# MLP products of a diffusion layer: eight half-sized block products against seven, in two phases

## The chip, the core and the metric

The kernel runs on one core of a Trainium2 chip. The metric is device time in microseconds (us) of one execution, as the median of three runs. Everything is float32. A product of two float32 operands is made of three TensorE passes: each operand is split into a rounded part (hi, type float32r) and the rest (lo), and hi·hi, hi·lo and lo·hi are added up in PSUM.

## What is computed

One layer over 512 latent tokens (and 256 context tokens) with 2048 features: modulated RMSNorm, a combined input projection that feeds three kinds of mixers, an output projection with gated residual, and then the part that this change is about, the MLP and the final norm:

```python
def _sq_relu_mlp(h, w1, w2):                      # h (512, 2048), w1 (2048, 8192), w2 (8192, 2048)
    a = jax.nn.relu(jnp.einsum('btd,df->btf', h, w1))
    return jnp.einsum('btf,fd->btd', a * a, w2)

# h = modulate(rmsnorm(x2), ...);  x = x2 + gate * mlp(h);  out = rmsnorm(x)
```

## The kernel before

TensorE holds 128x128 of one operand (the weight load, `PEld`) and streams columns of the other through it. `mm3` (L169 to L172) issues the three passes of a product, each with a weight load of its own.

Until about 1230 us of the profile the kernel does conditioning, input projection, mixers and output projection; the change leaves these as they are, but for the buffers that the output projection's end uses. Then come:

- The turn to the MLP (L921 to L946). `flip` scales and transposes the tokens `x2` by matmuls with the diagonal `dg` into PSUM tiles `pt`; ScalarE applies the modulation (`hf`, L944), VectorE rounds it into `hh` (L945), VectorE and GpSimd in turn form the rest `hl` (L946).
- The MLP loop over 8 groups of 1024 hidden units (`for g in range(NG)`, L950). In a group, 8 tiles of 128 hidden units are made from w1: the weights are held, `hh` and `hl` stream with 512 columns (all tokens), 16 row tiles by 3 passes into one PSUM bank `pa`. The bank goes through relu and square, and is split into `ah` and `al`, which stay in SBUF. Then the group's 1024 rows of w2 are used: `ah`/`al` are held (128 tokens), w2 streams with 512 columns into banks `yp`, and `add_up` multiplies by the gate `gb2` (L996) and adds into the residual `x2` (L997, on GpSimd).
- Both use `wunit` (L97): a unit is 128x1024 float32 (512 KB), loaded by SyncE's queue into one of three buffers `raw`, rounded on ScalarE (`whi`, L93) and subtracted on VectorE (`wlo`, L94), each with two buffers. `wunit` runs at a raised priority (`WPRI`), so the planner puts it ahead of other work of the same engine. Each engine executes its instructions in the order that the planner wrote.
- In the last group three of the four token tiles are finished first (`LASTM`), and the row of the fourth ends the kernel: gate, residual, sum of squares, `row_rstd`, scaling, two output DMAs (L1005 to L1010).

In all, w1 takes 64 tiles x 16 row tiles x 3 = 3072 matmuls of 512 columns and w2 the same number.

Of the kernel before, what the change touches and what calls it, by code (L numbers as in the profile page):

```python
# [9 lines left out]
F32 = mybir.dt.float32  # L10
# [7 lines left out]
P = 128  # L18
# [23 lines left out]
LASTM = (0, 1, 2)  # L42
GT = 8
# [5 lines left out]
def trunk_kernel(ctx: ExitStack, tc: tile.TileContext, a: dict, out: bass.AP, dbg: dict):  # L49
    """Products of float32 operands run as float32r passes: each operand is split exactly into  # L50
    hi (rounded to float32r) and lo = operand - hi, and hi*hi + hi*lo + lo*hi is accumulated."""
# [14 lines left out]
    gd = [dram.tile([P, 512], F32, name=f"gd{i}") for i in range(4)]  # L66

# [29 lines left out]
    def wunit(src, n, p=WPRI, after=None, into=None):  # L97
        """one unit of weights, loaded and split; `after` holds the load back until that is there"""
# [46 lines left out]
    def row_store(blk, ac):  # L145
        pb = mx.tile([P, 512], F32, tag="mx", name="pb")
        TE.matmul(pb, onem, ac, start=True, stop=True)
        S.copy(ac, pb)
        G.dma_start(out=gd[blk], in_=ac)
# [24 lines left out]
    def log1pexp(pool, tag, x, shape):  # L174
        """ln(1 + exp(-|x|))"""
# [6 lines left out]
    def rsqrt_into(y, t, v):  # L182
        """y = v ** -0.5: exponential of half the logarithm, then one Newton step"""
# [15 lines left out]
    hp = ctx.enter_context(tc.tile_pool(name="hT", bufs=1, side="right"))  # L199
# [14 lines left out]
    def col_rstd(rb, t, total, pb, n, start):  # L214
        """rsqrt of the mean over the features of every token's squares, on every partition"""
# [11 lines left out]
    with tc.tile_pool(name="pa", bufs=1) as pa:  # L227
# [8 lines left out]
        # four columns (c hi, c_ctx hi, c lo, c_ctx lo), repeated over the array's width  # L236
# [155 lines left out]
    def hg_b2(h, chain, mods):  # L392
        """q and output gate, feature-major"""
# [78 lines left out]
    def hg_gates(outs, tiles, toks):  # L472
        """log forget and key, token-major [tok, tile, fw|bw]"""
# [668 lines left out]
```

## Time and profile before

| | |
|---|---|
| median of three runs (lowest, highest) | 2671.26 us (2670.48, 2672.54) |
| span of the profiled execution | 2665.3 us |
| TensorE busy, weight loads busy | 98%, 84% |
| VectorE, ScalarE, GpSimd busy | 48%, 32%, 12% |
| moved by DMA | 349.61 MB, mean 131 GB/s |

The profiled execution is one of its own; between its span and the median of the runs lie 6.0 us, which hold what is before the first and after the last instruction. Ends of matmuls are modelled and overlap the next one, so a matmul's duration (0.39 us for 512 columns) is not its price; the price is the distance from one start to the next.

### The profile page before, as it was taken

What the parts mean: (1) busy time and instruction counts of PE and PEld (TensorE: products, weight loads), DVE (VectorE), ACT (ScalarE), POOL (GpSimd) and SP (SyncE); (2) the same over time, 40 slices, a digit from 0 to 9 for tenths busy, and PEclk for the clock granted to TensorE, in tenths of its full rate; (3) what the DMA queues carried; (4) which work ended last, traced back from release to release, by engine and by line L of the source; (5) the groups of instructions that cost most, each with busy time, mean ns of one, the idle gap of its engine ahead of it and who ended that gap; (6) DMA issues with size and microseconds to landing.
All of it is one profiled execution on the core that took longest, in us unless ns stands there. A gap on an engine that the chain in (4) does not pass through costs nothing.

```text
span 2665.3 us, 33283 instructions
## 1 busy us (share of the span) xinstructions
PE 2619.2 (98%) x13498; PEld 2248.4 (84%) x13498; DVE 1281.1 (48%) x1900; ACT 864.4 (32%) x1279; POOL 314.8 (12%) x301
## 2 busy tenths in 40 slices
PE   8999999999999999999999999999999999999998
PEld 6879999998999988787888888888888888888886
DVE  8885666755444556566333333333333333333345
ACT  7664445522222234223222212222122222221233
POOL 0030000001001010002011020120200201102014
PEclk9999999999999999999999999999999999999999
DMA  9843333435455464663322222222222222223234
GB/s 330 295 166 113 108 117 109 131 103 182 132 164 149 157 188 152 219 201 125 99 97 95 95 96 99 98 95 95 95 97 99 98 95 95 96 97 100 95 119 150
DMA packets 101099, 349.61 MB, mean 131 GB/s; under 512 B 15280, under 2 KB 15536, under 8 KB 100304
## 3 DMA queue, kind: packets, MB, share of 16 engines
q1 hardware_dynamic: 90000, 322.09, 36.3%
q0 software_dynamic: 10944, 25.39, 3.1%
q8 instruction: 106, 1.74, 0.3%
q14 instruction: 49, 0.40, 0.0%
HBM read 336.37 MB, written 11.01 MB: 130 GB/s over the span
## 4 chain that ended last, share of the span: by engine, by line
PE 79%; DMA 9%; DVE 7%; ACT 2%; issue 2%; POOL 1%; SPq 0%; DVEq 0%; ACTq 0%; POOLq 0%
PE pa L170 9%; PE pa L172 9%; PE pa L171 9%; PE yp L171 9%; PE yp L172 9%; PE yp L170 8%; DMA raw<-in_ada_dram 8%; DVE adac L119 3%; DVE wlo L94 2%; PE f L170 2%; PE f L171 2%; PE f L172 2%; PE vP L170 1%; PE vP L171 1%; PE vP L172 1%
## 5 line engine op out<-in xcount | busy, mean ns | idle before, releaser
L94 DVE TENSOR_TENSOR wlo<-raw,whi 128x1024 fp32r<-128x1024 f32 (+1 forms) x452 | 551.0, 1220 | 874.6 <-ACT whi L93 873.8
L93 ACT CAST whi<-raw 128x1024 fp32r<-128x1024 f32 (+1 forms) x452 | 466.0, 1036 | 1221.4 <-PE yp L172 564.9
L170 PE MATMUL pa<-hh,whi 128*128 128x512 f32 x1024 | 402.8, 393 | 0.0
L172 PE MATMUL pa<-hh,wlo 128*128 128x512 f32 x1024 | 401.8, 392 | 0.0
L171 PE MATMUL pa<-hl,whi 128*128 128x512 f32 x1024 | 398.0, 389 | 0.0
L171 PE MATMUL yp<-wlo,ah 128*128 128x512 f32 x960 | 373.9, 389 | 1.3 <-DVE wlo L94 1.3
L170 PE MATMUL yp<-whi,ah 128*128 128x512 f32 x960 | 373.9, 389 | 0.0
L172 PE MATMUL yp<-whi,al 128*128 128x512 f32 x960 | 373.6, 389 | 0.0
L997 POOL TENSOR_TENSOR x<-x,yt 128x512 f32<-128x512 f32 x124 | 190.0, 1562 | 1183.7 <-DVE yt L996 1170.1
L119 DVE SCALAR_TENSOR_TENSOR adac<-raw,csil,adac 128x512 f32<-128x512 f32 x256 | 192.0, 750 | 246.7 <-DMA raw<-in_ada_dram 237.4
L172 PEld LDWEIGHTS pa<-hh,wlo 128*128 128x128 f32 x1024 | 192.3, 188 | 44.5 <-DVE wlo L94 0.3
L171 PEld LDWEIGHTS pa<-hl,whi 128*128 128x128 f32 x1024 | 192.2, 188 | 43.5 <-POOL hl L946 0.3
L170 PEld LDWEIGHTS pa<-hh,whi 128*128 128x128 f32 x1024 | 192.5, 188 | 38.8
L171 PEld LDWEIGHTS yp<-wlo,ah 128*128 128x128 f32 x960 | 180.2, 188 | 40.0 <-DVE wlo L94 2.5
L170 PEld LDWEIGHTS yp<-whi,ah 128*128 128x128 f32 x960 | 180.2, 188 | 37.8 <-ACT whi L93 0.4
L172 PEld LDWEIGHTS yp<-whi,al 128*128 128x128 f32 x960 | 180.2, 188 | 37.5
L996 DVE TENSOR_TENSOR yt<-yp,gb 128x512 f32<-128x512 f32 x128 | 85.3, 687 | 51.2 <-PE yp L172 47.1
L170 PE MATMUL f<-whi,hh 128*128 128x384 f32 x256 | 90.7, 354 | 3.2 <-ACT whi L93 3.2
L171 PE MATMUL f<-wlo,hh 128*128 128x384 f32 x256 | 87.2, 341 | 0.6 <-DVE wlo L94 0.6
L172 PE MATMUL f<-whi,hl 128*128 128x384 f32 x256 | 86.9, 339 | 0.0
L170 PE MATMUL vP<-whi,hh 128*128 128x256 f32 x256 | 74.0, 289 | 0.0
L276 PE MATMUL ga<-whi,cw 128*128 128x256 f32 x256 | 66.4, 293 | 7.5 <-ACT whi L93 7.5
(365 smaller groups left out, 4330.1 us busy)
## 6 DMA issues: line engine op xcount, KB each, us to landing
raw<-in_w_dram SPq DMA_DIRECT2D x264, 512.0 KB, 3.5
raw<-in_ada_dram SPq DMA_DIRECT2D x192, 512.0 KB, 4.2
raw<-in_nb_dram SPq DMA_DIRECT2D x48, 512.0 KB, 3.5
raw<-in_wo_dram SPq DMA_DIRECT2D x32, 512.0 KB, 3.6
raw<-in_hb_dram SPq DMA_DIRECT2D x32, 384.0 KB, 3.1
wr<-in_hq_dram SPq DMA_DIRECT2D x16, 384.0 KB, 4.5
raw<-in_hb_dram SPq DMA_DIRECT2D x12, 512.0 KB, 3.5
xT<-in_xT_dram SPq DMA_DIRECT2D x4, 1024.0 KB, 11.1
```

What stands on the lines that cost most here:

```text
L93: S.copy(hi[:, :n], raw)
L94: V.tensor_sub(lo[:, :n], raw, hi[:, :n].bitcast(F32))
L119: V.scalar_tensor_tensor(ac, raw[:, kk * 512:(kk + 1) * 512], csil[:, 2 * u + kk:2 * u + kk + 1], ac, op0=ALU.mult, op1=ALU.add)
L170: TE.matmul(o, lh, rh, start=start, stop=False, skip_group_check=skip)
L171: TE.matmul(o, lh, rl, start=False, stop=False, skip_group_check=skip)
L172: TE.matmul(o, ll, rh, start=False, stop=stop, skip_group_check=skip)
L276: TE.matmul(ga[:, :256], st, hi[:, cs], start=(n == 0), stop=False)
L996: V.tensor_mul(t_, yp[m], gb2[:, cs])
L997: (V if end else G).tensor_add(x2[:, m, cs], x2[:, m, cs], t_)
```

## The change

The matrices of each product are cut in halves: the tokens in two times 256, the inner dimension in two, and the weights' columns in two. A block product of 2x2 by 2x2 blocks would take eight products of blocks. The new kernel makes seven, named N1 to N7, of sums of blocks; a fixed order (`visits`) interleaves two neighbouring blocks.

- Weights. N1, N2 and N3 load a block as it is (b11, b21, b22). N5, N6 and N4 use the buffer of N1 again: a DMA that GpSimd issues adds b12, then b22, then b21 onto what is there; N7 adds b12 onto the buffer of N3. Each of the seven is then split as before (`Weights.split`). The extra buffers are 3 raw and 3 split pairs in the first phase, 8 and 3 in the second.
- Phase 1 (w1): 32 blocks of 256 hidden units. A visit is 8 row tiles x 3 passes of 256 columns into one of the banks X, Y, Z; N6, N7 and N4 continue the sum that stands in bank X, N3 that in Y. After each visit ScalarE or VectorE takes the bank's state out. After N4: relu, square, four sums (`combine`), and a split into the seven operands of the next phase, which two DMAs write to DRAM (`acd`).
- Phase 2 (w2): 16 blocks of 512 hidden units by 1024 columns. A visit has two units of weights and two token tiles, 24 matmuls of 512 columns, and its operand (1 MB) is loaded from `acd` on every second block. After each visit VectorE adds to or subtracts from `y` (128x512, twice).
- The residual `x2` is kept in DRAM (`x2d`), and gate, residual and final norm come after the last block (`gate`, `finish_row`).
- The MLP's input is combined in the same way: for each of 8 pairs of row tiles two modulations, `combine`, and two splits (`hah`/`hal` 1024, `hbh`/`hbl` 768 columns).

```diff
-        hf = mlp.tile([P, T], F32R, tag="ah", name="hf", bufs=11).bitcast(F32)
-        S.activation(hf, pt.rearrange("p m t -> p (m t)"), AF.Identity, bias=mod[:, 0, k:k + 1], scale=mod[:, 1, k:k + 1])
-        V.tensor_copy(hh[:, k], hf)
-        (G if k % 2 else V).tensor_sub(hl[:, k], hf, hh[:, k].bitcast(F32))
+    def combine(x):
+        G.tensor_sub(x[:, 3], x[:, 6], x[:, 7])
+        V.scalar_tensor_tensor(x[:, 0], x[:, 3], -1.0, x[:, 4], op0=ALU.mult, op1=ALU.subtract)
+        G.tensor_sub(x[:, 1], x[:, 4], x[:, 7])
+        V.scalar_tensor_tensor(x[:, 2], x[:, 0], -1.0, x[:, 5], op0=ALU.mult, op1=ALU.subtract)
...
+        if k < 8:
+            hx = hc.tile([P, 8, 256], F32, tag="hx", name="hx", bufs=3)
+        S.activation(hx[:, 4:8:3] if k < 8 else hx[:, 5:7], pt, AF.Identity, bias=mod[:, 0, k:k + 1], scale=mod[:, 1, k:k + 1])
+        if k >= 8:
+            combine(hx)
+            S.copy(hah[:, :, p], hx[:, 3:7])
+            V.tensor_sub(hal[:, :, p], hx[:, 3:7], hah[:, :, p].bitcast(F32))
+            S.copy(hbh[:, :, p], hx[:, 0:3])
+            V.tensor_sub(hbl[:, :, p], hx[:, 0:3], hbh[:, :, p].bitcast(F32))
...
+        def operand(self, blk, name, src, held):
+            b11, b12, b21, b22 = src
+            with pri(WPRI):
+                if name in ("N1", "N2", "N3"):
+                    t = held[name] = self.raw()
+                    nc.sync.dma_start(out=t, in_={"N1": b11, "N2": b21, "N3": b22}[name])
+                else:
+                    t, add = {"N5": (held["N1"], b12), "N6": (held["N1"], b22), "N7": (held.get("N3"), b12),
+                              "N4": (held["N1"], b21)}[name]
+                    G.dma_start(out=t, in_=add, accum_op=ALU.add)
+                return self.split(t)
+
+    def visits(n):
+        out_ = [(0, "N1"), (0, "N5")]
+        for b in range(n):
+            more = b + 1 < n
+            out_ += [(b, "N2"), (b, "N3"), (b, "N6")] + [(b + 1, "N1")] * more + [(b, "N7")]
+            out_ += [(b + 1, "N5")] * more + [(b, "N4")]
+        return out_
...
+    for q, name in visits(32):
...
+        for k in range(8):
+            xh, xl = h_op(PLACE[name], k)
+            mm3(b_, wh[:, k], wl[:, k], xh, xl, new and k == 0, k == 7, skip=True)
+        with pri(EPRI):
+            if name in ("N1", "N5", "N3"):
+                r = made[q, name] = p1.tile([P, 256], F32, tag="r", name="r", bufs=4)
+                if name == "N1":
+                    S.copy(r, b_)
+                else:
+                    S.activation(r, b_, AF.Copy, scale=-1.0)
+            elif name == "N2":
+                ac[q] = p1.tile([P, 8, 256], F32, tag="ac", name="ac", bufs=1)
+                V.tensor_add(ac[q][:, 4], made[q, "N1"], b_)
+            elif name == "N6":
+                V.tensor_sub(ac[q][:, 5], made[q, "N3"], b_)
+            elif name == "N7":
+                V.tensor_sub(ac[q][:, 6], made[q, "N5"], b_)
+            else:
+                S.copy(ac[q][:, 7], b_)
+        if name == "N4":
+            x = ac[q]
+            S.activation(x[:, 4:8], x[:, 4:8], AF.Relu)
+            S.activation(x[:, 4:8], x[:, 4:8], AF.Square)
+            combine(x)
...
+            S.copy(xh, x[:, 0:7])
+            V.tensor_sub(xl, x[:, 0:7], xh.bitcast(F32))
+            for i, y in enumerate((xh, xl)):
+                nc.sync.dma_start(out=acd[q // 4].rearrange("o p i b t -> p o i b t")[:, :, i, q % 4], in_=y.bitcast(F32))
...
+    for b, name in visits(nb):
+        if j == 0:
+            t = aops[g, name] = p2.tile([P, 2, 4, 256], F32R, tag="ao", name="ao", bufs=8)
+            with pri(WPRI):
+                nc.sync.dma_start(out=t.bitcast(F32), in_=acd[g][PLACE[name]])
...
+                    mm3(bank[b, which][m], t[:, 0, i, sl], t[:, 1, i, sl], wh[:, kk], wl[:, kk], new and i == 0, i == 3, skip=True)
...
+        with pri(EPRI):
+            for m in range(2):
+                o = y[:, half + m, cs]
+                src = bank[b, which][m]
+                if first:
+                    S.activation(o, src, AF.Copy, scale=float(sign))
+                else:
+                    (V.tensor_add if sign > 0 else V.tensor_sub)(o, o, src)
```

## Rows read from the trace of the kernel before

**Rows 1.** The page: span, busy time of the engines, and its slices.

```profile
span 2665.3 us, 33283 instructions
...
PE 2619.2 (98%) x13498; PEld 2248.4 (84%) x13498; DVE 1281.1 (48%) x1900; ACT 864.4 (32%) x1279; POOL 314.8 (12%) x301
...
PEclk9999999999999999999999999999999999999999
```

**Rows 2.** Waits, 1200 to 2665 us: who waited, us in total, times, longest.

```profile
ACT whi L93 <- PE yp L172: 495.8, 119, 4.8
...
ACT whi L93 <- DMA raw<-in_w_dram: 10.2, 3, 4.9
```

**Rows 3.** The timeline of TensorE: first and last matmuls of the MLP.

```profile
1250.46 0.48 PE L170 MATMUL pa<-hh,whi 128*128 128x512 f32 x1
...
2653.52 0.40 PE L172 MATMUL yp<-hh,al 128*128 128x512 f32 x1
```

**Rows 4.** The timeline of TensorE where 256 columns stream: two runs of matmuls.

```profile
900.20 0.28 PE L171 MATMUL vP<-wlo,hh 128*128 128x256 f32 x1
...
901.34 0.28 PE L172 MATMUL vP<-whi,hl 128*128 128x256 f32 x1
...
902.16 0.28 PE L170 MATMUL vP<-whi,hh 128*128 128x256 f32 x1
...
904.90 0.28 PE L172 MATMUL vP<-whi,cl 128*128 128x256 f32 x1
```

**Rows 5.** Stretches: us, busy time by engine, granted clock, DMA share, GB/s.

```profile
10.00:20.00 10.00, 8.99 (x38) 5.64 (x37) 6.02 (x8) 7.85 (x15) 0.00 (x0) 1.00 1.01 424
...
50.00:60.00 10.00, 10.00 (x69) 9.18 (x68) 8.65 (x11) 7.11 (x9) 0.00 (x0) 1.00 0.96 355
...
1700.00:1800.00 100.00, 100.00 (x442) 82.63 (x441) 35.27 (x37) 21.59 (x22) 24.23 (x16) 1.00 0.29 95
```

**Rows 6.** Groups by line and shape, 1250 to 2660 us: busy, mean ns, idle before.

```profile
L94 DVE TENSOR_TENSOR wlo<-raw,whi 128x1024 fp32r<-128x1024 f32 x254 | 318.0, 1252 | 788.3 <-ACT whi L93 788.3
L93 ACT CAST whi<-raw 128x1024 fp32r<-128x1024 f32 x254 | 267.7, 1054 | 913.8 <-PE yp L172 482.2 <-PE pa L171 421.5 <-DMA raw<-in_w_dram 5.3
...
L996 DVE TENSOR_TENSOR yt<-yp,gb 128x512 f32<-128x512 f32 x128 | 85.3, 687 | 51.2 <-PE yp L172 47.1 <-POOL x L997 4.1
...
L962 ACT ACTIVATE rl<-pa 128x512 f32<-128x512 f32 x64 | 37.7, 589 | 0.0
```

**Rows 7.** The same view of 0 to 700 us and of GpSimd: smaller shapes.

```profile
L94 DVE TENSOR_TENSOR wlo<-raw,whi 128x768 fp32r<-128x768 f32 x32 | 30.5, 953 | 13.3 <-ACT whi L93 13.3
L93 ACT CAST whi<-raw 128x768 fp32r<-128x768 f32 x32 | 26.6, 830 | 57.0 <-PE f L172 47.6 <-DVE st L622 9.3
...
L352 POOL TENSOR_TENSOR cl<-cx,ch 128x256 fp32r<-128x256 f32 x8 | 7.1, 889 | 0.5 <-DVE cl L352 0.5
```

**Rows 8.** DMA issues: queue, count, KB each, median us to landing.

```profile
raw<-in_w_dram SPq DMA_DIRECT2D x264, 512.0 KB, 3.5
...
stg<-in_c_A_dram POOLq DMA_DIRECT2D x2, 512.0 KB, 4.1
...
gb<-in_fnw_dram SPq DMA_DIRECT2D x1, 1024.0 KB, 4.8
```

**Rows 9.** The timeline of the turn to the MLP, 1226 to 1264 us.

```profile
1229.76 0.39 PE L172 MATMUL yp<-whi,hl 128*128 128x512 f32 x1
...
1239.96 0.78 ACT L944 ACTIVATE hf<-pt,mod 128x512 f32<-128x512 f32 x1 [0.76 <-PE pt L931]
...
1241.57 10.14 ACT L944 ACTIVATE hf<-pt,mod 128x512 f32<-128x512 f32 x15
```

**Rows 10.** The timeline of the end, 2648 to 2666 us.

```profile
2653.95 0.69 DVE L996 TENSOR_TENSOR yt<-yp,gb 128x512 f32<-128x512 f32 x1 [2.06 <-PE yp L172]
2654.68 1.23 DVE L997 TENSOR_TENSOR x<-x,yt 128x512 f32<-128x512 f32 x1
...
2658.12 0.75 DVE L1006 SCALAR_TENSOR_TENSOR x<-x,fry,gb 128x512 f32<-128x512 f32 x1
```

More of the change, by code (lines that the diff above doesn't have):

```diff
@@ L863, in trunk_kernel @@
     ctx3.close()
[L866 removed]
+    ssq = adap.tile([P, 4, 4], F32, name="ssq")
+    ctxp = ExitStack()
+    post = ctxp.enter_context(tc.tile_pool(name="post", bufs=1, side="right"))
     x2 = post.tile([P, 4, D], F32, name="x2")
[L868 to L878 removed]
+    ctxy = ExitStack()
+    postb = ctxy.enter_context(tc.tile_pool(name="postb", bufs=1, side="right"))
+    gb = postb.tile([P, D], F32, name="gb")
+    ada = ada_units(range(12, 16), row_store)
+    for n in range(4):
+        ms = range(4)
         cs = slice(n * 512, (n + 1) * 512)
@@ new lines, in trunk_kernel, with h_op, __init__, raw @@
+    ctxc.close()
+    ctxp.close()
+    def h_op(o, k):
+        return (hah[:, o - 3, k], hal[:, o - 3, k]) if o >= 3 else (hbh[:, o, k], hbl[:, o, k])
+    class Weights:
+        def __init__(self, extra, n_raw, n_split, start=None):
+            self.extra, self.n_raw, self.n_split = extra, n_raw, n_split
+            self.raws = self.splits = 0
+        def raw(self):
+            i = self.raws % (3 + self.n_raw)
+            self.raws += 1
+            if i < 3:
+                return wp.tile([P, 1024], F32, tag="raw", name="raw", bufs=3)
+            return self.extra.tile([P, 1024], F32, tag="raw2", name="raw", bufs=self.n_raw)
+        def split(self, raw):
+            i = self.splits % (2 + self.n_split)
+            self.splits += 1
+            if i < 2:
+                return split(wp, raw, 1024, 2)
+            into = [self.extra.tile([P, 1024], F32R, tag=t + "2", name=t, bufs=self.n_split) for t in ("whi", "wlo")]
+            return split(None, raw, 1024, 2, into)
+        def operand(self, blk, name, src, held):
[9 more added lines that the diff above has]
+                return self.split(t)
@@ new lines, in trunk_kernel, with gate @@
+    ctx1.close()
+    ctxm.close()
+    ctxh_.close()
+    p2 = ctx.enter_context(tc.tile_pool(name="p2", bufs=1, reuse_waits="tile"))
+    wts = Weights(p2, 8, 3)
+    y = p2.tile([P, 4, D], F32, name="y")
+    gb2 = p2.tile([P, D], F32, name="gb2")
+    held, bank, aops = {}, {}, {}
+    z_done = []
+    def gate(m, n, end):
+        cs = slice(n * 512, (n + 1) * 512)
+        V.tensor_mul(y[:, m, cs], y[:, m, cs], gb2[:, cs])
+        V.tensor_add(y[:, m, cs], y[:, m, cs], xr[m][:, cs])
+        sq = p2.tile([P, 512], F32, tag="sq", name="sq", bufs=2)
+        S.activation(sq, y[:, m, cs], AF.Square, accum_out=ssq[:, m, n:n + 1])
+        if not end:
+            G.tensor_mul(y[:, m, cs], y[:, m, cs], fw[:, cs])
@@ new lines, in finish_row @@
+    def finish_row(m, n):
+        cs = slice(n * 512, (n + 1) * 512)
+        r = row_rstd(p2, m, m + 1)
+        V.scalar_tensor_tensor(y[:, m, cs], y[:, m, cs], r, fw[:, cs], op0=ALU.mult, op1=ALU.mult)
+        rest = [c for c in range(4) if c != n]
+        for c in rest:
+            c_ = slice(c * 512, (c + 1) * 512)
+            if c == rest[-1]:
+                V.tensor_scalar_mul(y[:, m, c_], y[:, m, c_], r)
+            else:
+                S.activation(y[:, m, c_], y[:, m, c_], AF.Copy, scale=r)
+        for c in range(2):
+            c2 = slice(c * 1024, (c + 1) * 1024)
+            nc.sync.dma_start(out=out[m * P:(m + 1) * P, c2], in_=y[:, m, c2])
```

215 lines of the change are left out of this document (106 added, 109 removed).

## The prediction

> **What bounds the kernel now.** The page comes first: TensorE is busy 98% of a span of 2665.3 us at full granted clock in every slice [rows 1]. Busy time overstates a pipelined engine, so the next views are the waits and the stretches. In the MLP, 1250 us to the end, ScalarE's rounding of weights waits for TensorE to free its buffers (495.8 us for those of w2 alone) and hardly ever for a load, 10.2 us [rows 2]: weights are always ahead, and TensorE sets the pace. The timeline gives that pace from start to start: the first MLP matmul starts at 1250.46 and the last at 2653.52 [rows 3], 1403 us for 6144 matmuls, 0.228 us each. In that stretch the DMA engines are busy to 0.29 [rows 5], VectorE and ScalarE to a third or less. So the MLP holds 1403 of 2665 us, is bound by streamed columns, and has room beside it; the question is how much of that room the new work takes.
>
> **The change part by part.**
>
> *Matmuls.* Phase 1: 32 blocks x 7 visits x 24 = 5376 matmuls of 256 columns. Phase 2: 16 x 7 x 24 = 2688 of 512 columns. Columns fall by exactly one eighth, but phase 1 has more matmuls, each with a weight load, for fewer columns each. What 256 columns cost stands in the mixers: from 900.20 to 901.34 ten starts, 0.114 us each; from 902.16 to 904.90 twenty-three, 0.119 us [rows 4]. I take 0.117, near the longer run. Phase 1: 5376 x 0.117 = 629 us (613 to 640). Phase 2: 442 starts in 100 us give 0.227 in the w2 part [rows 5]: 2688 x 0.227 = 610. Sum 1239 against 1403: -164 us (-153 to -180).
>
> A rule against a row: the Trainium skill, "TensorE: Matmul & The Clock Gate", section "Back-to-back issue gap", puts the gap at N / 2.4 + 2.5 ns, 109 ns for 256 columns; phase 1 would then take 587 us, an estimate by that page, and the time would be 42 us shorter. The trace's 0.114 to 0.119 speaks against it, as does 0.227 for 512, where the rule has 0.216.
>
> *Weights: the pace that is needed.* A visit of phase 1 lasts 24 x 0.117 = 2.8 us and eats one unit; before, a unit lasted twice that. A block of seven lasts 19.7 us. ScalarE: 7 x 1.05 for rounding [rows 6], four extractions of 256 columns at some 0.4 (589 ns for 512), relu and square of 1024 at about 1.05, the split of 1792 columns about 1.8: 12.7 us. VectorE: 7 x 1.25, three extractions and two sums at some 0.4, 2.2 for the split: 13 us. Both fit, two thirds busy. GpSimd has two sums at 0.89 [rows 7] and four DMA issues. In phase 2 a visit is 24 x 0.227 = 5.4 us and wants two units, 2 x 1.25 + 2 x 0.69 = 3.9 us on VectorE [rows 6]; a block is 38.1 us.
>
> *DMA bandwidth.* The densest stretch of the trace moves 424 GB/s at a DMA share of 1.01 [rows 5]. A unit is 0.524 MB. A block of phase 1 loads three units (1.57 MB), adds four onto buffers (2.10 MB) and writes 2 x 7 x 128 KB (1.84 MB) to DRAM: 5.5 MB, 13.0 us at that rate, if an adding DMA costs what a copy does. A block of phase 2 loads six units (3.15 MB), adds eight (4.19 MB) and loads 3.67 MB of operands: 11.0 MB, 26.0 us. No DMA of the trace adds, so its price is bounded: not under one copy, since the same bytes come and go; it must also read what it adds to, a second copy's worth; at most I allow three copies (two reads and a write, one after the other). With price p in copies, a block takes 8.0 + 4.95p us in phase 1 and 16.1 + 9.9p in phase 2. At two, nearest to what it does, that is 17.9 of 19.7 and 35.9 of 38.1 us: still hidden, with only a tenth to spare. I take two.
>
> For this price there is a page: the Trainium skill, "Collectives: The Full Stack", section "Why 7× under link rate — side-by-side accounting", says that the add is free but the two source reads halve the rate (ratio 1.93). By it a block takes 17.5 and 35.2 us, and the sum stays. No run here shows it yet.
>
> *DMA latency.* N5 can be added only after N1 has been split, N6 after N5, N4 after N6. One such link is a rounding and a subtraction (1.05 + 1.25) [rows 6] and an adding DMA: 512 KB by GpSimd's queue land in 4.1 us [rows 8], plus 1.24 for the second read: 7.7 us. In the worst order two links stand in series in one block (N5 to N6, then N1 to N5 of the next): 2 x 7.7 + 1.05 = 16.4 of 19.7 us. Each may find ScalarE at the 1.8 us copy, VectorE at the 2.2 us one, or GpSimd waiting for `combine`'s input. If a link is late, the waiting `wlo` stands at the head of VectorE, and the extraction behind it is late too; N7 and N4 continue a bank that was read only one visit (2.8 us) before, so TensorE then stops. I charge 1 us per block of phase 1 and 0.2 in phase 2, where the chain needs 16.4 of 38.1: 35 us in all (0 if everything is early; two links of 10.7 would make the cycle 22.4, 86 us).
>
> *The turn into phase 1.* Now 20.7 us lie between the last projection matmul (1229.76) and the first of w1, while modulations take about 0.68 us each [rows 9]. After: 8 pairs, each 2 x 0.68 + 1.05 + 0.83 = 3.2 us on ScalarE (copies of 1024 and 768 [rows 6, 7]), with hand-overs to GpSimd and VectorE some 3.6: 29 us from 1240, to 1269. N1 needs all eight pairs; its other seven parts, 2.5 us, are done by then. So the MLP starts as if at 1266.5: +16 us (10 to 22).
>
> *Between the phases.* Phase 2's buffers lie where phase 1's were, so the first operand (1 MB, 4.8 us [rows 8]) and its split weights wait for the last matmuls; N5's link of 7.7 us then has only N1's 5.4 us to hide behind. +10 us (3 to 20).
>
> *The end.* Two rows end the kernel instead of one, with an extraction more (0.69) and VectorE's work of 0.69 + 1.23 + 0.75 [rows 10] for the first row, most of it under the second row's 2.7 us of matmuls: +4 us (2 to 6). GpSimd's adds into the residual go, and cost nothing now; VectorE's extractions take their place within the budget above. The writes of `x2d`, 4 MB or 10 us of DMA, lie under the turn.
>
> **Sum.** 2665.3 - 164 + 16 + 10 + 4 + 35 = 2566 as a span; with the 6.0 us that lie around it, 2572 us.
>
> **The rivals.**
>
> *DMA sets the pace at price two.* For: 17.9 and 35.9 us hold only at 424 GB/s, and right after, at a share of 0.96, the trace moves 355 [rows 5]. At 355 GB/s a block of phase 1 takes 21.4 us and of phase 2 42.9: 32 x 1.7 + 16 x 4.8 = +131 in place of the 35, so 2668 us; a rate halfway gives about 2610. Against: that stretch had waits of its own between loads.
>
> *Slower: an adding DMA costs about three copies.* Then a block takes 22.9 and 45.8 us, +3.2 x 32 + 7.7 x 16 = 225 in place of 35: 2762 us. It turns into a loss once what DMA adds exceeds 35 + 99 us, at p = 2.7 (6.7 us of all DMA engines per 1 MB added, where a copy takes 2.5). Against: the add works on bytes as they pass; for: no row shows any.
>
> *It doesn't save what it says.* If 256 columns cost as much as half of 0.228 plus a weight load that no longer hides, phase 1 would keep its old time; the rows at 0.114 to 0.119 with a weight load each exclude all but 11 us of that, which is in the range.
>
> **How the numbers follow.** This kernel can be told from no change at about 0.2%, 5 us. The forecast, TensorE's pace with small stalls (2520 to 2615): 0.47. DMA's pace at price two (2615 to 2666): 0.27. The same rival's end within 5 us of 2671: 0.05. Price near three: 0.21, about half of it above 2700. Under 2520 would need no stalls, no turn and the 0.114: 0.03 of the forecast's share. So faster 0.74, same 0.05, slower 0.21. The range takes in the second case and the lower part of the third: 2520 to 2700.
>
> **What would show each step.** In the new profile: starts of phase 1's matmuls 0.117 us apart and 0.227 in phase 2; phase 1 near 660 us and phase 2 near 615; adding DMAs landing in 5 to 8 us; DMA shares of 0.85 to 0.95 in both phases. If DMA binds, ScalarE's rounding waits for adding DMAs instead of TensorE, and the share stands at 1 while TensorE has gaps; landings then grow well past 8 us. If the forecast's stalls are the wrong kind, TensorE waits for extractions of N6 and N7 with DMA below 0.9. What would make the prediction wrong most is the price of the add, which enters both phases with 158 us per copy once past about 2.3 copies.

## The result and the profile after

The changed kernel takes 2755.85 us (median of four runs, 2751.75 to 2756.55), against 2671.9 us of the kernel before in the same measurement: a ratio of 1.0311, 95% interval 1.0296 to 1.0325. It is 3.1% slower. The profiled execution has a span of 2754.1 us, 1.8 us under the median.

Lines of the page after: busy times, slices, one queue, the head of the chain that ended last, and DMA issues (queue, count, KB each, median us to landing).

```profile
span 2754.1 us, 39051 instructions
PE 2549.1 (93%) x15418; PEld 2303.1 (84%) x15418; DVE 1618.6 (59%) x2264; ACT 1154.0 (42%) x1595; POOL 393.6 (14%) x507
...
PEclk9999999999999999998999999999998999999998
DMA  8843333435545556664898888898879999999995
...
q0 software_dynamic: 48128, 160.67, 28.3%
...
PE 27%; DMA 13%; issue 5%; ACT 4%; DVE 4%; POOL 0%; ACTq 0%; DVEq 0%; POOLq 0%; SPq 0%
...
raw<-in_w_dram POOLq DMA_DIRECT2D x256, 512.0 KB, 8.7
...
raw<-in_w_dram SPq DMA_DIRECT2D x192, 512.0 KB, 8.2
ao<-acd SPq DMA_DIRECT2D x56, 1024.0 KB, 9.5
```

Against [rows 1], TensorE falls from 98% to 93% busy. DMA, at 0.29 in the old MLP [rows 5], stands mostly at 8 and 9 tenths from slice 20 on. A load that landed in 3.5 us [rows 8] takes 8.2, and an adding DMA 8.7. DMA holds 13% of the chain.

The timeline gives the two phases: first and last matmul of phase 1, then of phase 2 (start us, duration, engine, line).

```profile
1273.55 0.56 PE L171 MATMUL pa<-hh,whi 128*128 128x256 f32 x1
...
2068.62 0.28 PE L173 MATMUL pa<-hh,wlo 128*128 128x256 f32 x1
...
2086.05 0.77 PE L171 MATMUL yp<-whi,ao 128*128 128x512 f32 x1 [17.15 <-DMA ao<-acd]
...
2737.52 0.39 PE L173 MATMUL yp<-whi,ao 128*128 128x512 f32 x1
```

Phase 1 lasts 795 us and phase 2 651.5: together 1446, where the MLP before took 1403 [rows 3], although an eighth of the columns is gone. The same two stretches by engine (busy time, granted clock, DMA share, GB/s):

```profile
1273.00:2069.00 796.00, 699.96 (x5381) 691.87 (x5379) 418.44 (x429) 388.29 (x458) 157.29 (x196) 0.93 0.85 220
2086.00:2738.00 652.00, 630.32 (x2688) 513.32 (x2688) 412.92 (x464) 244.97 (x267) 123.46 (x136) 0.97 0.97 274
```

No engine but TensorE is over two thirds busy in either. DMA is at 0.85 and 0.97, and TensorE's granted clock is down to 0.93 and 0.97. The waits of phase 1 (who waited for what, us in total, times, longest):

```profile
POOL raw L1017 <- DVE wlo L95: 457.1, 128, 12.1
ACT whi L94 <- DMA raw<-in_w_dram: 215.0, 70, 6.8
...
POOL ac L938 <- ACT ac L1066: 167.8, 31, 10.6
ACT whi L94 <- PE pa L172: 161.9, 56, 5.9
PE pa L171 <- DVE ac L1058: 84.1, 29, 6.7
```

Before, ScalarE's rounding waited for weights 10.2 us in the whole MLP [rows 2]; now 215 us in phase 1 alone, more than for TensorE to free its buffers (161.9). TensorE, though, stops almost only at one place: at N7's first matmul, for N6's extraction on VectorE (L1058), 29 times in 32 blocks.

One such stop, from the timeline of the changed kernel:

```profile
1622.24 0.42 DVE L1058 TENSOR_TENSOR ac<-r,pa 128x256 f32<-128x256 f32 x1
1622.57 2.36 DVE L95 TENSOR_TENSOR wlo<-raw,whi 128x1024 fp32r<-128x1024 f32 x2
...
1625.23 0.85 POOL L1017 DMA_DIRECT2D raw<-in_w_dram  x1 [5.63 <-DVE wlo L95]
...
1635.37 1.05 ACT L94 CAST whi<-raw 128x1024 fp32r<-128x1024 f32 x1 [3.84 <-DMA raw<-in_w_dram]
1636.32 0.37 ACT L1062 COPY ac<-pa 128x256 f32<-128x256 f32 x1
...
1637.81 1.06 ACT L1066 ACTIVATE ac<-ac 128x1024 f32<-128x1024 f32 x1
1639.02 0.74 POOL L938 TENSOR_TENSOR ac<-ac 128x256 f32<-128x256 f32 x1 [5.37 <-ACT ac L1066]
...
1641.36 1.69 ACT L1070 CAST xh<-ac 128x1792 fp32r<-128x1792 f32 x1
...
1643.09 2.03 DVE L1071 TENSOR_TENSOR xl<-ac,xh 128x1792 fp32r<-128x1792 f32 x1 [0.60 <-ACT xh L1070]
...
1645.03 1.22 DVE L95 TENSOR_TENSOR wlo<-raw,whi 128x1024 fp32r<-128x1024 f32 x1
...
1646.50 0.42 DVE L1058 TENSOR_TENSOR ac<-r,pa 128x256 f32<-128x256 f32 x1
...
1647.06 0.36 PE L171 MATMUL pa<-hbh,whi 128*128 128x256 f32 x1 [2.38 <-DVE ac L1058]
```

It reads downwards. Behind N6's extraction (L1058) VectorE makes two `wlo`, and for these GpSimd waits before it issues an adding DMA at 1625.23. ScalarE's rounding gets that DMA's data at 1635.37, 10 us later. N4's extraction (L1062) stands behind that rounding on ScalarE and is late with it. From it hang relu and square, `combine` on GpSimd and VectorE, and the split of 1792 columns (L1070, L1071). On VectorE, N6's extraction stands behind that split and one more `wlo`, so N7, which continues N6's bank, starts at 1647.06, 2.66 us after the matmul before it. That is 24.26 us after the same matmul of the previous block (1622.80); the forecast's cycle was 19.7.

So a loop closes, from N6's extraction to that of the next block, with one late add in it and the end of the block in series behind it. The same four events can be followed through 29 neighbouring blocks of phase 1, from the second on. The means are 3.0 us from N6's extraction to the issue of the add, 9.7 from issue to landing (8.9 to 10.4), 1.05 until N4's extraction starts, and 10.5 from there to the next extraction of N6: 24.2 us, the length of a block. When the add is issued at 1625.23, four other DMAs are in flight, and the last of these lands at 1631.66. The DMA engines are full until the late data are there, and then nearly idle while the split of the block's end runs (columns as above):

```profile
1622.20:1639.20 17.00, 16.40 (x124) 16.43 (x125) 6.82 (x8) 5.82 (x7) 2.71 (x4) 0.90 1.05 258
1640.00:1644.00 4.00, 4.00 (x36) 4.00 (x35) 3.30 (x4) 3.69 (x4) 1.30 (x2) 1.00 0.12 48
```

Behind a stop TensorE also runs at the lower of its two levels for a while. The stretches behind the stop that ended at 1622.80 (columns as above):

```profile
1622.80:1624.20 1.40, 1.40 (x11) 1.40 (x12) 1.40 (x2) 0.00 (x0) 0.00 (x0) 0.95 1.10 211
1624.30:1627.20 2.90, 2.90 (x15) 2.90 (x15) 0.62 (x1) 0.12 (x1) 0.85 (x1) 0.50 1.03 280
1627.50:1634.00 6.50, 6.50 (x56) 6.50 (x56) 2.67 (x3) 1.96 (x3) 1.68 (x2) 1.00 1.05 299
```

Between 1624.30 and 1627.20 the granted clock is 0.50, 1.2 GHz of 2.4, and 13 matmuls start in 2.9 us, where full clock has one every 0.12.

Counting starts over the whole of phase 1: 5376 x 0.120 = 645 us; 36 distances over 1 us, 104 us in all; 467 distances between 0.16 and 0.35, most of them 0.213, which cost 43 us beyond the 0.120; the rest 8. In phase 2: 2688 x 0.227 = 610, and 42 us of stops and slow stretches.

### The profile page after: what moved, and what is told of

Same layout as the page of the kernel before. It is cut to its first block, busy times and chain, and to the rows that moved or that the text cites. A ratio compares the mean times of both kernels' runs of the same rounds, so it can differ in the third digit from the quotient of the medians.

```text
span 2754.1 us, 39051 instructions
## 1 busy us (share of the span) xinstructions
PE 2549.1 (93%) x15418; PEld 2303.1 (84%) x15418; DVE 1618.6 (59%) x2264; ACT 1154.0 (42%) x1595; POOL 393.6 (14%) x507
## 3 DMA queue, kind: packets, MB, share of 16 engines
q0 software_dynamic: 48128, 160.67, 28.3%
## 4 chain that ended last, share of the span: by engine, by line
PE 27%; DMA 13%; issue 5%; ACT 4%; DVE 4%; POOL 0%; ACTq 0%; DVEq 0%; POOLq 0%; SPq 0%
DMA raw<-in_w_dram 12%; PE yp L172 5%; PE yp L173 5%; PE yp L171 5%; PE pa L171 4%; PE pa L172 4%; PE pa L173 4%; ACT whi L94 2%; DVE wlo L95 2%; ACT xh L1070 2%; DVE ac L1056 0%; DVE ac L1058 0%; DMA ao<-acd 0%; DVE y L1090 0%; DVE y L1089 0%
## 5 line engine op out<-in xcount | busy, mean ns | idle before, releaser
L95 DVE TENSOR_TENSOR wlo<-raw,whi 128x1024 fp32r<-128x1024 f32 (+1 forms) x644 | 777.4, 1213 | 546.4 <-ACT whi L94 535.5
L171 PE MATMUL yp<-whi,ao 128*128 128x512 f32 x896 | 356.0, 397 | 30.9 <-DMA ao<-acd 17.1
L172 PE MATMUL yp<-wlo,ao 128*128 128x512 f32 x896 | 355.8, 397 | 7.8 <-DVE wlo L95 7.8
L1017 POOL DMA_DIRECT2D raw<-in_w_dram x256 | 216.0, 844 | 991.2 <-DVE wlo L95 953.0
L173 PE MATMUL yp<-whi,ao 128*128 128x512 f32 x896 | 353.7, 395 | 0.0
L171 PE MATMUL pa<-hbh,whi 128*128 128x256 f32 x768 | 238.3, 310 | 87.5 <-DVE ac L1058 84.1
L171 PE MATMUL pa<-hh,whi 128*128 128x256 f32 x1024 | 292.9, 286 | 6.1 <-ACT hh L975 3.1
L172 PE MATMUL pa<-hl,whi 128*128 128x256 f32 x1024 | 292.8, 286 | 2.3 <-DVE hl L976 2.3
L173 PE MATMUL pa<-hh,wlo 128*128 128x256 f32 x1024 | 291.9, 285 | 0.0
L172 PE MATMUL pa<-hbl,whi 128*128 128x256 f32 x768 | 235.0, 306 | 0.0
L173 PE MATMUL pa<-hbh,wlo 128*128 128x256 f32 x768 | 234.5, 305 | 0.0
L171 PEld LDWEIGHTS yp<-whi,ao 128*128 128x128 f32 x896 | 171.4, 191 | 71.9 <-ACT whi L94 29.5
L173 PEld LDWEIGHTS yp<-whi,ao 128*128 128x128 f32 x896 | 171.7, 192 | 36.0
```

Of the source, the lines that this page charges most:

```text
L95: V.tensor_sub(lo[:, :n], raw, hi[:, :n].bitcast(F32))
L171: TE.matmul(o, lh, rh, start=start, stop=False, skip_group_check=skip)
L172: TE.matmul(o, lh, rl, start=False, stop=False, skip_group_check=skip)
L173: TE.matmul(o, ll, rh, start=False, stop=stop, skip_group_check=skip)
L1017: G.dma_start(out=t, in_=add, accum_op=ALU.add)
```

## The experiments

Phases are from first to last matmul start; "share" is DMA's. Runs with an interval were executed four times, the others once.

| run | us | ratio to before | phase 1 | share | phase 2 | share |
|---|---|---|---|---|---|---|
| kernel before | 2671.9 | 1 | MLP 1403 | 0.29 [rows 5] | | |
| changed kernel | 2755.85 | 1.0296 to 1.0325 | 795 | 0.85 | 651.5 | 0.97 |
| e1_copies | 2632.8 | | 701.5 | 0.74 | 618 | 0.81 |
| e2_ac2 | 2752.99 | | 796 | | 648 | |
| e3_early_end | 2756.36 | | 797 | | 651 | |
| e4_pool_sums | 2710.89 | 1.013 to 1.0164 | 750 | 0.52 | 655 | 0.97 |
| e5_few_writes | 2711.39 | | 749 | 0.75 | 666 | 0.96 |
| e6_short_end | 2745.52 | | 783 | 0.90 | 651 | 0.97 |
| e7_pool_short_end | 2703.24 | | 722 | 0.54 | 653 | 0.97 |
| e8_far_order | 2859.91 | 1.0685 to 1.0721 | 895.5 | 0.43 | 651 | 0.98 |
| e9_far_and_loads | 2842.28 | 1.0631 to 1.0663 | 896 | 0.43 | 629.5 | 0.84 |
| e10_half_adds | 2656.15 | 0.993 to 0.9963 | 711 | 0.78 | 627 | 0.85 |
| e11_half_adds_v | 2634.74 | 0.9847 to 0.988 | 689 | 0.81 | 628 | 0.85 |
| e12_short_end_v | 2783.48 | | 828 | 0.83 | 647 | 0.98 |

**Is it the adding?** The same DMAs, waits and bytes, but as copies.

```diff
-                    G.dma_start(out=t, in_=add, accum_op=ALU.add)
+                    G.dma_start(out=t, in_=add)
```

> Leaves out the adding: the 256 DMAs of GpSimd's queue that add a block onto a buffer only overwrite it, same bytes, same waits, same order (so the products are of other sums). Theory A (the second read of an adding DMA, 328 ns per 4 KB row against 159, loads the DMA engines and makes landings long): without it a block of phase 1 falls from 24.3 us at the densest to 20 or 21 (phase 1 from 795 to 640 to 680 us), landings from 8.7 to about 5.5 us, phase 2 from 651 to 610 to 620 us, DMA share from 0.85 and 0.98 to about 0.65 in both; time 2570 to 2620 us. Theory B (the order of the extractions and the single buffer ac, whatever a DMA costs): phase 1 stays above 750 us, time above 2700 us.

Measured: 2632.8 us, 123 us less. Its stretches, a row of its page on the queue and one on its DMA issues:

```profile
1277.00:1979.00 702.00, 663.30 (x5380) 655.53 (x5378) 416.15 (x429) 389.56 (x457) 118.41 (x196) 0.98 0.74 250
1996.00:2615.00 619.00, 613.60 (x2688) 506.48 (x2688) 418.35 (x465) 248.60 (x267) 85.46 (x136) 0.99 0.81 289
...
q0 software_dynamic: 48128, 160.67, 18.7%
...
raw<-in_w_dram POOLq DMA_DIRECT2D x256, 512.0 KB, 5.2
```

Time and phase 1 are 13 and 21 us above theory A's bounds; theory B's (above 2700 and 750) are farther off. The add itself costs 94 us of phase 1 and 33 of phase 2. Its price in DMA time can be read from the queue: 28.3% of 2754.1 less 18.7% of 2631.0 is 287 us over 256 adds, 1.12 us of all DMA engines each, beside 1.24 us for a copy of 0.524 MB at 424 GB/s [rows 5]: price 1.9. In the packet records a row of 4 KB takes 327 ns where it is added (median, phase 2 of the changed kernel) and 159 where it is copied (median here): 2.06. The price is two, not three. Even so phase 1 stays 40 us over its forecast of 661 with copies. The loop above shows why: its other parts stay (3.0, 1.05 and 10.2 us), while this DMA lands in 7.1 us instead of 9.7, and the 29 blocks take 21.4 us instead of 24.2.

**Is it the end of the block as such?** Two edits that take pressure from relu to the split: a second buffer `ac` (`r` gives up one), and the end of the block at raised priority.

```diff
-                ac[q] = p1.tile([P, 8, 256], F32, tag="ac", name="ac", bufs=1)
+                ac[q] = p1.tile([P, 8, 256], F32, tag="ac", name="ac", bufs=2)
```

> Two buffers ac instead of one (and three r instead of four, for the room), so that the extraction of N2 and N6 needn't wait for the split of the block before. Theory B (the single buffer holds up N6's extraction, and N7 waits for it): the 84 us that TensorE waits for N6's extraction go, with the half clock behind them, phase 1 falls to about 690 us, time about 2650 us. Theory A (the late adding DMA behind it sets the block): the wait moves to another place, phase 1 stays within 20 us of 795, time 2735 to 2760 us.

```diff
-            S.activation(x[:, 4:8], x[:, 4:8], AF.Relu)
...
+            with pri(EPRI):
+                S.activation(x[:, 4:8], x[:, 4:8], AF.Relu)
...
```

> Relu, square, combine and split at the end of a block of phase 1 get the priority of the extractions (EPRI), ahead of the rounding of weights. Theory B (the end of a block stands behind roundings that wait): phase 1 falls by 50 to 100 us, time 2660 to 2710 us. Theory A: the planner's order changes little of what waits for adding DMAs; within 25 us of 2756 us, to either side.

Measured: phase 1 of 796 and 797 us, the times 2752.99 and 2756.36. Both are inside theory A's bounds. The single buffer is not what holds the block. What the order of instructions costs these runs do not show, since they left it as it was: in both traces N6's extraction still stands on VectorE behind the split of 1792 columns and one `wlo` (split at 1618.64, extraction at 1621.72 in e2_ac2).

**Without adding DMAs in phase 1.** GpSimd sums the blocks in SBUF; each of the four is loaded once (five extra `raw` buffers, and `r` gives up one).

```diff
+                        held[n_] = self.raw()
+                        nc.sync.dma_start(out=held[n_], in_=blk_)
...
+                    if add:
+                        G.tensor_add(held[t], held[t], held[add])
```

> Phase 1 alone: the four blocks are each loaded once by SyncE's queue (four loads per block instead of three loads and four adding DMAs), and GpSimd forms the four sums in SBUF; five extra raw buffers instead of three, r three instead of four. Phase 2 as it is. Theory A: DMA share in phase 1 falls to about 0.5, no rounding waits for a landing, and phase 1 comes to 650 to 700 us if GpSimd's sums (about 3 us each, 12 of 20 us per block) don't slow VectorE by more than a third; time 2610 to 2660 us, faster than the kernel before. Theory B: phase 1 stays above 750 us; time above 2710 us.

Measured: 2710.89 us, phase 1 of 750 us at a DMA share of 0.52. Theory A's bounds are missed; theory B's (750 and 2710) lie right at the result. So 45 us go with the adds, but DMA at half its load still leaves 89 us over the forecast. What came in their place stands in the groups of VectorE and GpSimd (count, busy us, mean ns):

```profile
L1083 DVE TENSOR_TENSOR xl<-ac,xh 128x1792 fp32r<-128x1792 f32 x31 | 110.3, 3557 | 24.9 <-ACT xh L1082 24.9
...
L1020 POOL TENSOR_TENSOR raw<-raw 128x1024 f32<-128x1024 f32 x127 | 310.1, 2443 | 336.5 <-DVE wlo L95 249.1 <-DMA acd<-xl 79.2 <-DMA raw<-in_w_dram 8.1
```

GpSimd's sum takes 2.44 us, and VectorE's split of 1792 columns beside it 3.56 us, where it took 2.03 in the timeline above.

**Fewer bytes.** The writes of `acd` only for the first four blocks of phase 1; phase 2 reads those.

```diff
-            for i, y in enumerate((xh, xl)):
+            for i, y in enumerate((xh, xl)) if q < 4 else ():
```

> Leaves out 28 of the 32 pairs of writes to acd in phase 1 (phase 2 reads the first group's operands eight times); the adding DMAs stay. The writes hold a DMA share of 0.23 of phase 1. Theory A1 (an adding DMA lands late because the DMA engines are loaded by other transfers): landings of the adds in phase 1 fall from 8.7 to 6 to 7 us and phase 1 from 795 to 690 to 730 us. Theory A2 (it lands late by its own price and the turns it takes): landings stay above 8 us, phase 1 above 770 us. Phase 2 within 10 us of 651 in both.

Measured: phase 1 of 749 us at a share of 0.75, between the bounds of A1 and A2; phase 2 of 666 us, outside its own. The adds are all there and still cost two copies, but 46 us of phase 1 go. What adds and writes have in common is the DMA engines: between 1300 and 2000 us the adds now land in a median of 6.8 us, in the changed kernel in 7.8. That is inside A1's 6 to 7 us.

**A shorter end.** The end of the block is cut: what N2, N6 and N7 leave in `ac` is rectified, squared and split right behind N7, N4's goes through relu on its way out of PSUM, and only 1024 columns hang from N4. `ac` has two buffers.

```diff
+        if name == "N7":
+            x = ac[q]
+            S.activation(x[:, 0:3], x[:, 0:3], AF.Relu)
+            S.activation(x[:, 0:3], x[:, 0:3], AF.Square)
...
+            S.copy(xh7[q][:, 4:7], x[:, 0:3])
+            V.tensor_sub(xl7[q][:, 4:7], x[:, 0:3], xh7[q][:, 4:7].bitcast(F32))
```

> Adding DMAs as they are. The end of a block of phase 1 is made shorter: three of the four quarters go through relu, square and split before N4, the last one takes relu out of PSUM directly, extraction buffers are two and of their own; what follows N4 falls from 8.3 to about 5.5 us of work. Theory C (a late add and the end of the block stand in one cycle, so each us saved at the end comes off the block): phase 1 falls by 32 x 2 to 3 us, to 700 to 735 us, time 2660 to 2695 us. Theory A alone (the lateness of the adds sets the block): phase 1 above 770 us, time above 2730 us.

Measured: phase 1 of 783 us at a share of 0.90: 12 us. Theory C is missed; the bounds of theory A alone hold. With the sums on GpSimd instead of by DMA (the edit of e4_pool_sums) and b11 and b21 in buffers of their own, the same cut:

```diff
+                        if n_ in ("N1", "N2"):
+                            held[n_] = self.extra.tile([P, 1024], F32, tag="raw" + n_, name="raw", bufs=2)
```

> The sums of phase 1 on GpSimd as in the run before with that name, and the short end of a block; raw buffers seven, by the role of the block. Theory C: phase 1 falls from 750 (sums on GpSimd alone) to 650 to 690 us, time 2610 to 2650 us. Theory D (GpSimd's sums of 2.4 us slow VectorE and stand ahead of combine, and that is what is left): phase 1 stays above 720 us, time above 2680 us.

Measured: phase 1 of 722 us, 28 less than e4_pool_sums; the time falls by only 8 us, since phase 1 starts at 1293 instead of 1273 (the first load of the new buffers waits) and phase 2 is untouched. Phase 1 and time are as theory D has them; theory C is missed. So the cut is worth 12 us with four adding DMAs, and 28 without them, the other buffers included. That late adds and the chain behind them each hide part of what the other costs would fit this, but is not shown.

**More visits between dependent sums.** Another order of visits, with GpSimd's sums and the shorter end. Between N6 and N7 lie four visits instead of one, between N7 and N4 two instead of one; between N5 and N3, which continues N5's bank, it is one instead of two.

```diff
+            for d, name in ((0, "N1"), (0, "N5"), (1, "N7"), (0, "N3"), (0, "N6"), (1, "N4"), (0, "N2")):
+                if 0 <= b - d < n:
+                    out_.append((b - d, name))
```

> Phase 1 as in the run with GpSimd's sums and the short end, but in another order of visits (N1, N5, N7 of the block before, N3, N6, N4 of the block before, N2): between N6 and N7 lie four visits instead of one, between N7 and N4 two; the first two loads go to buffers that are free early. Theory E (what is left of phase 1's excess is that a product continues a bank one visit after its last state was taken out, and VectorE takes it out late): the 2 us gap at N7 of each block goes, phase 1 falls from 722 to 650 to 675 us with the first matmul at 1273 again, time 2620 to 2650 us. Theory D (GpSimd's sums and their clash with VectorE): phase 1 stays above 700 us, time above 2670 us.

Measured: 2859.91 us, phase 1 of 895.5 us at a DMA share of 0.43. The expectation is missed by far, and on the wrong side. The wait has moved:

```profile
PE pa L171 <- ACT r L1077: 161.7, 31, 6.2
```

TensorE now waits for N5's extraction, 31 times and 5.2 us on the mean, each time at N3, where the new order has put the visits closer together. ScalarE makes it, in line with roundings that wait 168.2 us for GpSimd's sums and with `xh`, which waits 126.4 us for `combine`. So with less than half of DMA's time in use, phase 1 can be 100 us longer than in the changed kernel. Against e7_pool_short_end, 174 us less, only the order of visits and the assignment of buffers differ; which of the two costs how much is not shown.

**Phase 2 alone.** As e8_far_order, and in phase 2 N5 and N7 are summed by GpSimd from one load of b12; N6 and N4 stay adding DMAs.

```diff
+                    if name in ("N5", "N7"):
+                        G.tensor_add(t, t, held["b12"])
+                    elif name in ("N6", "N4"):
+                        G.dma_start(out=t, in_=b22 if name == "N6" else b21, accum_op=ALU.add)
```

> As e8_far_order, and in phase 2 the two sums with b12 (N5 and N7) are made by GpSimd from one load, so that of eight adding DMAs per block four stay (ten extra raw buffers, seven operand buffers ao instead of eight). Theory A (phase 2 is set by the DMA engines, 39.7 us busy of 40.7 per block): the load falls to about 32 us per block, the share to 0.82, and phase 2 from 651 to 613 to 622 us, as with copies; time 2580 to 2615 us. If GpSimd's sums slow VectorE's work instead: phase 2 stays above 640 us.

Measured: phase 2 of 629.5 us instead of 651, between the two bounds; phase 1 is unchanged at 896, so the time, 2842.28 us, is far off theory A's. Phase 2 by engine, and ScalarE's wait for weights in it:

```profile
2193.00:2822.00 629.00, 618.34 (x2686) 507.37 (x2687) 478.08 (x457) 249.48 (x260) 224.00 (x136) 0.99 0.84 258
...
ACT whi L94 <- DMA raw<-in_w_dram: 5.7, 3, 3.5
```

In the changed kernel the same wait holds 139.1 us of phase 2. Halving the adds brings DMA's share from 0.98 to 0.84 and takes 21 us. The buffers changed with it (ten extra `raw` instead of eight, seven `ao` instead of eight), so that it is DMA's time alone rests on e1_copies, where nothing but the adding was left out and 33 us went.

**Both halves in both phases.** The original order of visits, the shortened end of e6_short_end, and in both phases the lines of e9_far_and_loads: two sums by GpSimd and two by DMA.

> In both phases the weight sums of N5 and N7 are made by GpSimd from one load of their two blocks, while those of N6 and N4 stay adding DMAs (the copy kept, the second block added by a DMA), in the order of visits of the changed kernel, with the shortened end of a block of phase 1 and early buffers for the first block. So two blocks in a period are added by DMA instead of four, and GpSimd makes two sums of about 2.4 us in a period instead of four. Theory F (two things fill a period of phase 1 together, the DMA time of the adding packets and the in-order engines that wait for a late add; halving both brings the period near TensorE's pace): phase 1 680 to 700 us, phase 2 about 630 us as in e9_far_and_loads, time 2620 to 2650 us, under the kernel before. Rival (the clash of GpSimd's sums with VectorE's subtractions, and the in-order extraction behind them, stay whatever number of adds is left): phase 1 above 720 us as in e7_pool_short_end, time above 2660 us; with that phase 1 and the phase 2 of e9_far_and_loads the time would be about 2663 us, within half a per cent of the kernel before.

Measured: 2656.15 us, phase 1 of 711, phase 2 of 627. It is faster than the kernel before (0.993 to 0.9963). Theory F's time is missed by 6 us and its phase 1 by 11; the rival's bounds (above 720, above 2660) are missed too, so a part of each holds. Behind the last matmul this kernel takes 22.7 us and the changed one 16.5, which is as much as the 6 us in time. TensorE's stops stand at N7's first matmul again, 30 times for N6's extraction (37.4 us). What that extraction comes behind, in the timeline of this kernel:

```profile
1904.44 0.42 ACT L1107 ACTIVATE ac<-ac 128x256 f32<-128x256 f32 x1
1904.54 3.30 POOL L1023 TENSOR_TENSOR raw<-raw 128x1024 f32<-128x1024 f32 x1 [2.65 <-DVE wlo L95]
...
1907.80 0.74 POOL L1108 TENSOR_TENSOR xa<-ac 128x256 f32<-128x256 f32 x1
```

`combine` (L1108) has its input at 1904.86 and stands 2.9 us behind a weight sum on GpSimd.

**`combine` off GpSimd.** Its two differences go to VectorE, in e10_half_adds and in e6_short_end.

```diff
-            G.tensor_sub(xa[:, 3], x[:, 2], x[:, 3])
+            V.tensor_sub(xa[:, 3], x[:, 2], x[:, 3])
...
-            G.tensor_sub(xa[:, 1], x[:, 0], x[:, 3])
+            V.tensor_sub(xa[:, 1], x[:, 0], x[:, 3])
```

> As e10_half_adds, but the two differences of `combine` in phase 1 that GpSimd made are made by VectorE (128x256 each, some 0.4 us), so GpSimd has only weight sums and adding DMAs. In e10_half_adds TensorE still stops about 1.4 us in each block ahead of N7: `combine` waits for GpSimd from 1904.89 to 1907.80 behind a weight sum of 3.30 us, and N6's extraction on VectorE comes behind what follows. Theory G (that place behind GpSimd is all that is left of the stall): the gap goes, phase 1 from 711 to 665 to 685 us, the time 2610 to 2630 us. Rival (the adds by DMA that remain, or VectorE itself, end the cycle): phase 1 stays above 700 us, the time above 2645 us.

Measured: 2634.74 us, phase 1 of 689 us, 22 less. Theory G was right in kind: the distances over 1 us between matmul starts of phase 1 fall from 55 us in all to 27. Its bounds are missed by 5 us in time and 4 in phase 1; the rival's are missed too. VectorE pays for part of it:

```profile
1530.68 3.30 POOL L1023 TENSOR_TENSOR raw<-raw 128x1024 f32<-128x1024 f32 x1 [2.64 <-DVE wlo L95]
1531.64 2.63 DVE L1108 TENSOR_TENSOR xa<-ac 128x256 f32<-128x256 f32 x1
...
1534.19 0.41 DVE L1110 TENSOR_TENSOR xa<-ac 128x256 f32<-128x256 f32 x1
```

The first difference lasts until 0.3 us after the end of GpSimd's sum; the same shape behind it takes 0.41 us. This version beats both kernels: 1.2 to 1.5% under the kernel before, and 121 us under the changed one.

> As e6_short_end (all weight sums by adding DMAs, shortened end of a block, phase 1 of 783 us), with the two differences of `combine` in phase 1 on VectorE instead of GpSimd. Theory (with four adding DMAs in a block it is the late landing that ends the cycle, since ScalarE's rounding waits 254.8 us for loads and adds there): phase 1 stays within 12 us of 783, the time within 12 us of 2745. Rival (the hand-over to GpSimd in the end of a block ends the cycle there too): phase 1 falls below 750 us, the time below 2715 us.

Measured: 2783.48 us, phase 1 of 828 us. Both expectations are missed: it is 45 us longer than e6_short_end. The timeline:

```profile
1656.86 0.42 DVE L1078 SCALAR_TENSOR_TENSOR xa<-xa,ac 128x256 f32<-128x256 f32 x1
...
1660.54 1.05 ACT L94 CAST whi<-raw 128x1024 fp32r<-128x1024 f32 x1 [6.13 <-DMA raw<-in_w_dram]
1661.49 1.05 ACT L1079 CAST xh<-xa 128x1024 fp32r<-128x1024 f32 x1
```

The sums that `xh` (L1079) needs are ready at 1657.28, but the planner has put `xh` behind the rounding of a weight that an adding DMA brings late, at 1660.54; in e6_short_end it stood ahead of it (1614.21, the rounding at 1617.01). On an engine that works in order, a late add costs what stands behind it, and that is a matter of where the planner puts it. That the new order is the whole of the 45 us is argued, not shown; ScalarE's wait for weights grew from 254.8 to 386.9 us.

## Why the prediction was wrong, step by step

| | forecast | measured | difference |
|---|---|---|---|
| phase 1 starts | 1266.5 | 1273.6 | +7 |
| phase 1 | 629 + 32 = 661 | 795 | +134 |
| between the phases | 10 | 17.4 | +7 |
| phase 2 | 610 + 3 = 613 | 651.5 | +38 |
| last matmul to the end | 11.8 + 4 = 15.8 | 16.6 | +1 |
| around the span | 6.0 | 1.8 | -4 |

Together +183 us on 2572, which is the 2755 measured. Point by point, in the order of the prediction:

- *Matmuls.* Phase 2's 0.227 was right to the digit. Phase 1's starts are 0.120 apart, not 0.117: the long run of [rows 4], 0.119, was the better end, and the choice below it cost 16 us. The formula that was set against the rows, 109 ns, stands in the Trainium skill, "TensorE: Matmul & The Clock Gate", section "Back-to-back issue gap", for an isolated matmul and not for a stream; the 0.120 of this stream speaks against it as the rows did. The saving is there: 645 + 610 = 1255 us of streaming in place of 1403.
- *The price of the add.* Two copies was right: 327 against 159 ns a row, and 1.9 by the queue's time. The Trainium skill, "Collectives: The Full Stack", section "Why 7× under link rate — side-by-side accounting", has 1.93 for the adding step of a collective; the trace agrees for a sum onto SBUF.
- *DMA bandwidth.* The rate was the wrong one. Everything was priced at the 424 GB/s of the densest 10 us [rows 5]. DMA was busy 0.85 x 795 / 32 = 21.1 us per block of phase 1 and 0.97 x 651.5 / 16 = 39.5 us of phase 2, where 17.9 and 35.9 were forecast; counted by the same bytes that is 360 and 385 GB/s. "A tenth to spare" was not there. In phase 1 even 0.85 hides the pattern: full for 17 us of the block shown, nearly idle for 4. In phase 2 e9_far_and_loads took 21 of the 38 us with half of the adds (and other buffers), and e1_copies, with half of the DMA time of all the adds gone, 33.
- *DMA latency: the step that failed.* It took 5.3 us for an adding DMA, from two copies that landed in 4.1 us [rows 8] (at 188 us of the trace, behind a stretch with a DMA share of 0.18), for a state that the bandwidth step itself put at 0.9. In the changed kernel adds land in 7.8 us in phase 1 and 9.9 in phase 2, and the one on which a block of phase 1 hangs in 9.7. A bound for late landings was written down (two links of 10.7 make the cycle 22.4, 86 us over 32 blocks), yet only 32 us were charged for phase 1.
- *What stands behind a late link.* The chain was another one, too. The prediction named the extraction behind `wlo` on VectorE, but put two links in series and treated the end of the block as a load on each engine beside them. The timeline shows one link and the end of the block in series: late add, rounding, N4's extraction behind it, relu to split, N6's extraction behind that, and from there two `wlo` to the next add. That is 14.5 us of work and waiting on the engines and 9.7 of landing, 24.2 us. With the forecast's 5.3 in place of the 9.7 the same chain would take 19.9 us (an estimate from these numbers), TensorE's own pace; so it is the landing that makes it show, with 4 us a block where 1 was charged.
- *The lower clock.* No term stood for it. The stops bring matmuls 0.213 us apart behind them: 43 us in phase 1. In the loop above they are no cost of their own: N4's extraction, which the loop passes through, begins about 1 us or more after the end of N4's last matmul in 31 of 32 blocks (1633.16 and 1636.32 in the one shown). At full clock the stop would have been longer instead; that is argued from the order, no run shows it.
- *The turn.* Its size was near: 33.3 us from the last projection matmul (1240.25) to the first of phase 1 (1273.55), forecast 36.7 (1229.76 to 1266.5). But it begins 10.5 us later than before (1240.25 against 1229.76 [rows 9]), for which no term stood. Matmul by matmul the changed kernel is 1.2 us late at 13 us of the profile, 3.4 at 703 and 9.1 at 1053, in the part that the change leaves as it is; no run here tells why.
- *Between the phases* it was 17.4 us, inside its bounds of 3 to 20; the first operand is late, [17.15 <-DMA ao<-acd].

Of the rivals, *price three* gave 2762 us, 6 us from the result, and is wrong: the price was two, and the 225 us it put on DMA's time came from other places. *DMA's pace at price two* is right for phase 2 in kind, with half its size. In phase 1 DMA is full for most of a block and then waits itself, so the pace is that of the loop. (That rival's "rate halfway gives about 2610" is a wrong sum: at 390 GB/s a block takes 19.5 and 39.0 us, which gives about 2550.) The prediction's own sign for "stalls of the wrong kind" (TensorE waits for extractions of N6 and N7 with DMA below 0.9) is what phase 1 shows.

The range ended at 2700 since the case of a loss was tied to the price of an add alone. The charge for the latency, 35 us, should have been worked out at the landings of a loaded DMA, and then the sum would have been at 2572 - 32 + 86 = 2626 with the bound as written; with the 24.8 us that a block took on the mean it would have been 2572 - 32 + 32 x 5.1 = 2703, a loss.

What stays open: e11_half_adds_v is 106 us under the changed kernel in phase 1, by fewer adds, a shorter end and `combine` on VectorE together. One at a time, on the changed kernel, no adds gave 45 us, the shorter end 12, and `combine` on VectorE beside the shorter end lost 45; the shares don't add up, and how the 106 us divide isn't known. Untested is the other half of the loop: N6's extraction ahead of the split on VectorE, with the adds as they are.

## What to carry to other kernels

DMA's share alone does not give a landing time. In the trace of before, a stretch as full as the new phases had loads that landed in a median of 5.1 us, where the changed kernel's loads took 8.2 (10 to 70 us: the stretch, and its loads with count, KB and median us to landing):

```profile
10.00:70.00 60.00, 55.57 (x324) 45.08 (x323) 50.82 (x64) 45.32 (x62) 0.00 (x0) 1.00 0.93 343
...
raw<-in_ada_dram SPq DMA_DIRECT2D x25, 512.0 KB, 5.1
```

The late add of the block shown had four other DMAs in flight ahead of it, two of them loads and one a write; without most of the writes (e5_few_writes) adds landed in 6.8 us instead of 7.8. So list, for the one DMA on which a loop hangs, what is in flight ahead of it, and follow what stands behind the waiting instruction on each in-order engine, round the whole loop, before calling a link hidden. An operation that DMA does "on the way" (an add) costs DMA time and latency like a second copy; splitting such sums between DMA and an idle engine was better here than either alone, 711 us against 783 and 722 with the same end of the block, though not the same buffers. An engine that takes over work in a loop should not also sit in the loop's longest chain: here that was worth 22 us, while the same edit without the halved adds lost 45, with another order of the planner.

## What the runs showed of the hardware

- A DMA that adds onto SBUF takes 327 ns for a row of 4 KB, a copying one 159 ns (medians, changed kernel and e1_copies); GpSimd needs 0.84 us to issue the former (L1017, mean of 256) and 0.54 the latter.
- VectorE and GpSimd get in each other's way. GpSimd's sum of 1024 columns takes 2.4 us, and 3.30 where it meets VectorE; VectorE's difference of 256 columns takes 2.63 instead of 0.41 us, its split of 1792 columns 3.56 instead of 2.03. An extraction on VectorE with one input in PSUM took 0.42 us at 1522.22 of e11_half_adds_v, in the middle of a GpSimd sum (1521.35, 2.39 us), and so did all 31 that met one. The Trainium skill, "SBUF — State Buffer", section "Who interferes with whom", says that a VectorE instruction with two SBUF inputs contends with a GpSimd instruction that reads SBUF, and one with at most one SBUF input does not; these rows agree.
- After a stop of 4 us (the block shown) TensorE started 11 matmuls, 0.12 us apart but for the second; then came 16 distances of 0.21 us, at a granted clock of 0.50, 1.2 GHz of 2.4, and then 1.00 again. Nothing in the prediction stood for that; over phase 1 the mean granted clock is 0.93.
